# One decoder layer on one core: 192 transfers of the mixer issued from GpSimd's queue in place of the sync engine's

## The chip, the cores and the metric

The kernel runs on one core of one Trainium2 chip. Its time is the device time of one execution in microseconds (us). The engines are TensorE (PE, with its weight loads as PEld), VectorE (DVE), ScalarE (ACT), GpSimd (POOL) and the sync engine (SP). Each has a queue of its own, works through it in order, and waits at its head on semaphores. A DMA is issued by an instruction in one of these queues; its issue takes time on that engine, and the transfer then runs on the core's 16 DMA engines.

## The reference

One inference step of one layer, for 1024 prompt tokens and 8 sample tokens, all in float32: a half-step SwiGLU, a token mixer, cross-attention, a second half-step SwiGLU. The change lies in the mixer:

```python
proj = h @ P['w_in']                      # one projection, its columns split into the parts below
# RWKV-7 time mixing, 16 heads of 64: r, k, v, decay, a, g from token-shifted columns
S = S * w + sa * (kk * a) + v * k ;  y = S r            # per token, a scan over the prompt
rwkv_out = (groupnorm(y) + bonus) * g
# RG-LRU: conv of width 4, block-diagonal gates, linear scan
lru_out = hs * gelu(p_gelu)
gates = sigmoid(p_gate)
merged = gates[0] * rwkv_out + gates[1] * lru_out
out = merged @ P['w_mix_out']
h = layer_norm(alpha * h + out)
```

## The kernel before

Activations lie channels on partitions, 1032 columns wide (1024 prompt tokens and 8 samples). GEMMs take the columns in thirds of 344 (`CH3`). A float32 product is made of three matmuls on split operands (`mm3`, lines 122 to 127): a high part `HH` and a rest `HL` of the activations, `wh` and `wl` of the weights, which ACT and DVE split as the weights land in `raw` (lines 94, 99, 100).

The mixer's main loop runs over 16 units: 8 pairs of 128-channel tiles taken two at a time, each in 4 pieces of 256 or 264 tokens. For one unit there are small matmuls, ACT and DVE work and few POOL instructions: `stage` (token shift, norms, decays), `inverse` (a triangular solve), `chain` (the state carried from unit to unit, `ch`, `y`, `QZ`, `wsb`, lines 1105 to 1123) and `branch` (RG-LRU, lines 1005 to 1050, and the merge). POOL raises sums to the power -0.5 for the norms (`ivs`, `ivc`, line 798), copies `BN` (line 894), and does the same power in the samples (`v`, `w`, lines 1150 and 1220). A norm is a small matmul with ones (line 795), a DVE step, the power on POOL, ACT's scaling by the result, and a PE transposition of that (line 804).

Between these steps GEMMs are woven in as filler (`gemms`). `project` makes one 128-channel tile of the input projection: per third a GEMM into PSUM (`g`), an evacuation by ACT into `ev` (three buffers), and a store of it to DRAM `GD` (line 644), from where the units load it back later. The main loop makes 50 such tiles, 150 stores. The `lora` tiles, 18 stores ahead of the loop, go through the same line with `then` unset. Behind the last tile of the projection stands the output projection. `merged` loads the merged columns `MG` of a third, six 128-channel tiles, into `ev` (line 1241), and `direct` splits each into `HH` (ACT) and `HL` (DVE); `out_proj` multiplies them, eight output tiles by three thirds, 18 matmuls each, and stores the results to `FD` (line 1257). The buffers `ev` of project, merged and out_proj are the same three, used in turn.

What lies in each engine's queue, and in which order, is settled when the program is built: a scheduler takes the woven steps and puts each engine's instructions in order, also by which queue a transfer is issued from. Before the change SP issues all DMAs of the mixer: weights, the units' loads and stores (`T`, `D`, `GD`, `MG`), and the three named above.

Of the kernel before, what the change touches and what calls it, by code (L numbers as in the profile page):

```python
# [543 lines left out]
def mixer(octx, S, I, O, MG, HD, pre):  # L544
# [5 lines left out]
    nc, tc = S.nc, S.tc  # L550
# [7 lines left out]
    with ExitStack() as ctx:  # L558
# [66 lines left out]
        FD = S.dram.tile([8, 128, NT], F32, name="FD")  # L625
        GD = [S.dram.tile([128, 12, NT], F32, name="GD%d" % p) for p in range(8)]

        def cols(w, c0, n, q, kt=KT):
            yield from settled(S, c0, n)
            for k in range(kt):  # L630
                mm3(nc, q, wblock(w, k), S.HH[:, k, c0:c0 + n], S.HL[:, k, c0:c0 + n], k == 0, k == kt - 1)
                if k % 2:
                    yield

        def project(p, mt, gi, func, sc, w, cs, psg, pool, then=None):

            for c0, n in cs:
                q = psg(n)
                yield from cols(w, c0, n, q)
                if then:  # L640
                    then(c0, n)
                e = pool.tile([128, 344], F32, tag="ev", name="ev", bufs=3 if then else 2)[:, :n]
                ACT(e, q, func, scale=sc)
                nc.sync.dma_start(out=GD[p][:, gi, c0:c0 + n], in_=e)

        def tiles(p):

# [13 lines left out]
        def gemms():  # L661
# [18 lines left out]
            for j, (p, x, i) in enumerate(todo[:-1]):  # L680
                yield from project(p, *x, W[j], CH3, psg, t1, load)
                ready.add((p, x[1]))
                if i in (2, 5):
                    ends(p, i == 2)
# [4 lines left out]
            def then(c0, n):  # L689
                load(c0, n)  # L690
                merges.append(merged(c0, n))

            for _ in project(p, *x, W[len(todo) - 1], CH3, psg, t1, then):
                for m in merges:
                    next(m, 0)
                yield
            ready.update(((p, x[1]), "h"))
            yield from out_proj(W[len(todo):], load, merges)


        with ExitStack() as c2:
# [16 lines left out]
            def first():  # L718

                w = [S.ahead] + [load_split(S, I["w_in"][mt]) for mt in (25, *(x[0] for x in tiles(0)[:2]))]  # L720
                for cs in ([c] for c in CH3):
                    for i in range(2):
                        yield from low_in(i, w[i], cs)
                    for i in range(2):
                        yield from project(0, *tiles(0)[i], w[2 + i], cs, psl, lp)
# [62 lines left out]
        def tmp(tag, n=264, bufs=1, pool=None):  # L788
            return (pool or (t1 if tag in LATE else ta)).tile([128, n], F32, tag=tag, name=tag, bufs=bufs)
# [265 lines left out]
        def direct(k, c0, n, e):  # L1055

            ACT(S.HH[:, k, c0:c0 + n], e)
            TTo(S.HL[:, k, c0:c0 + n], e, S.HH[:, k, c0:c0 + n].bitcast(F32), ALU.subtract)
# [175 lines left out]
        def merged(c0, n):  # L1234

            for k in range(KT - 2):
                while not all(("mg", k, j) in ready for j in range(5) if c0 < (NT if j == 4 else 256 * j + 256) and
                              256 * j < c0 + n):
                    yield
                e = tmp("ev", 344, 3)[:, :n]  # L1240
                nc.sync.dma_start(out=e, in_=MG[k, :, c0:c0 + n])
                direct(k, c0, n, e)
                if k % 2:
                    yield

        def out_proj(W, load, merges):

            for m in range(KT):
                for j, (c0, n) in enumerate(CH3):
                    if m == 0:  # L1250
                        yield from merges[j]
                    q = psg(n)
                    yield from cols(W[m], c0, n, q, KT - 2)
                    load(c0, n)
                    e = tmp("ev", 344, 3)[:, :n]
                    ACT(e, q, scale=1.0 / ALPHA)
                    nc.sync.dma_start(out=FD[m, :, c0:c0 + n], in_=e)

        def out_last(n, w, st_, tags=(("g", 2),)):

# [63 lines left out]
        for t in range(nu):  # L1324
            g, n = divmod(t, 4)
# [417 lines left out]
```

## Time and profile before

| | us |
|---|---|
| median of three runs | 3201.08 (3195.89 to 3203.86) |
| profiled execution | 3202.45, its span 3200.7 |
| PE busy | 3015.8 (94%) |
| DVE busy | 2198.6 (69%) |
| ACT busy | 1434.0 (45%) |
| POOL busy | 558.1 (17%), 526 instructions |
| mixer's main loop with projection tiles as filler | about 850 to 1840 |
| first merged load to the last of them split | 1841 to 1917 |
| DMAs, all of one hardware kind of queue | 382.69 MB, 40.4% of 16 engines' span |

A busy time is the sum of an engine's instructions, register, branch and DMA-issuing instructions left out. An engine's busy share is a mean over stages, so the windows below are read stage by stage. The clock is the one granted to TensorE, as a share of 2.4 GHz. The profiled execution lies 1.4 us over the median.

### The profile page before, as it was taken

Reading aid. Unit: us, or ns where it says so; the run is one execution under the profiler, and the core shown is the slowest. Engines: PE = TensorE matmul, PEld = TensorE weight load, DVE = VectorE, ACT = ScalarE, POOL = GpSimd, SP = SyncE. Lnnn points to the kernel's source line nnn. Section 1 sums busy time; section 2 is a strip of 40 time slices with the busy share of each in tenths; the row PEclk is TensorE's granted clock in tenths of the full one; section 3 lists DMA queues with packets and bytes.
Section 4 is the critical chain, followed back from the end, with each engine's and each line's share of the span. In section 5 each row is a group of like instructions: output and inputs, shape, how many; then the busy total and the mean of one; then the engine's idle time right before and its main releaser. Section 6 shows DMA issues by size and latency. Waiting matters only on the chain. (4 is left out here: it accounts for less than half of the span.)

```text
span 3200.7 us, 63254 instructions
## 1 busy us (share of the span) xinstructions
PE 3015.8 (94%) x23324; PEld 2848.3 (89%) x23324; DVE 2198.6 (69%) x5903; ACT 1434.0 (45%) x3195; POOL 558.1 (17%) x526
## 2 busy tenths in 40 slices
PE   8999999999999999999999979889897999999997
PEld 8999999999888888888878858778887999999997
DVE  7666665574366887777777877776678666666556
ACT  5333352125465565556455655364235433334212
POOL 2222200132010011010001000260005322220111
PEclk9999999999999999999998969899999999999998
DMA  4222253314644554545554455554543222225321
GB/s 138 80 80 78 79 162 107 111 48 140 205 126 132 148 145 137 137 126 155 138 146 115 129 140 153 172 181 128 153 120 125 71 80 80 80 80 159 107 86 54
DMA packets 391301, 386.72 MB, mean 121 GB/s; under 512 B 153904, under 2 KB 292176, under 8 KB 390992
## 3 DMA queue, kind: packets, MB, share of 16 engines
q1 hardware_dynamic: 390992, 382.69, 40.4%
q8 instruction: 183, 3.00, 0.4%
q14 instruction: 126, 1.03, 0.1%
HBM read 277.54 MB, written 105.23 MB: 120 GB/s over the span
## 5 line engine op out<-in xcount | busy, mean ns | idle before, releaser
L125 PE MATMUL ps<-HH,wh 128*128 128x258 f32 (+1 forms) x2384 | 718.6, 302 | 18.7 <-ACT HH L510 7.8
L126 PE MATMUL ps<-HL,wh 128*128 128x258 f32 (+1 forms) x2384 | 716.7, 301 | 0.0
L127 PE MATMUL ps<-HH,wl 128*128 128x258 f32 (+1 forms) x2384 | 715.7, 300 | 0.0
L125 PE MATMUL g<-HH,wh 128*128 128x344 f32 (+2 forms) x1840 | 624.5, 340 | 15.9 <-DVE ql L1435 4.2
L127 PE MATMUL g<-HH,wl 128*128 128x344 f32 (+2 forms) x1840 | 596.8, 325 | 1.0 <-DVE wl L100 1.0
L126 PE MATMUL g<-HL,wh 128*128 128x344 f32 (+2 forms) x1840 | 594.3, 324 | 0.6 <-POOL HL L215 0.4
L125 PEld LDWEIGHTS ps<-HH,wh 128*128 128x128 f32 x2384 | 451.4, 189 | 21.0 <-ACT HH L510 7.8
L126 PEld LDWEIGHTS ps<-HL,wh 128*128 128x128 f32 x2384 | 451.2, 189 | 0.4 <-DVE HL L511 0.3
L127 PEld LDWEIGHTS ps<-HH,wl 128*128 128x128 f32 x2384 | 450.4, 189 | 0.0
L125 PEld LDWEIGHTS g<-HH,wh 128*128 128x128 f32 x1840 | 357.1, 194 | 35.3 <-DVE ql L1435 5.5
L126 PEld LDWEIGHTS g<-HL,wh 128*128 128x128 f32 x1840 | 357.7, 195 | 5.3 <-POOL HL L215 1.4
L127 PEld LDWEIGHTS g<-HH,wl 128*128 128x128 f32 x1840 | 356.1, 194 | 5.1 <-DVE wl L100 1.3
L228 ACT ACTIVATE wh<-raw 128x512 fp32r<-128x512 f32 x280 | 176.4, 631 | 322.2 <-PE ps L126 262.7
L334 POOL TENSOR_TENSOR raw<-raw 128x512 f32<-128x512 f32 x160 | 214.0, 1337 | 566.6 <-DVE wl L229 383.2
L229 DVE TENSOR_TENSOR wl<-raw,wh 128x512 fp32r<-128x512 f32 x280 | 206.7, 739 | 138.6 <-ACT wh L228 131.8
L100 DVE TENSOR_TENSOR wl<-raw,wh 128x512 fp32r<-128x512 f32 x302 | 218.6, 731 | 100.6 <-ACT wh L99 98.3
L99 ACT ACTIVATE wh<-raw 128x512 fp32r<-128x512 f32 x302 | 184.6, 625 | 222.5 <-PE ps L126 76.0
L442 DVE SCALAR_TENSOR_TENSOR acc<-ps,acc 128x344 f32<-128x344 f32 x336 | 168.4, 512 | 141.1 <-PE ps L127 140.4
L551 DVE TENSOR_TENSOR pr<-tq,iv 128x2 f32<-128x2 f32 (+30 forms) x496 | 160.8, 324 | 3.2
L556 ACT ACTIVATE ev<-g 128x344 f32<-128x344 f32 x192 | 86.9, 453 | 136.8 <-PE g L127 132.0
L949 DVE TENSOR_REDUCE tq<-pr 128x1 f32<-128x2 f32 (+30 forms) x496 | 121.8, 246 | 2.9
L556 ACT ACT_TABLE_LOAD x93 | 119.3, 1283 | 6.9 <-DVE cs L551 2.9
(404 smaller groups left out, 6302.8 us busy)
## 6 DMA issues: line engine op xcount, KB each, us to landing
raw<-in_wi_dram SPq DMA_DIRECT2D x176, 256.0 KB, 2.9
raw<-in_w_in_dram SPq DMA_DIRECT2D x116, 256.0 KB, 3.2
GD<-ev SPq DMA_DIRECT2D x168, 172.0 KB, 1.9
raw<-in_wo_dram SPq DMA_DIRECT2D x104, 256.0 KB, 2.8
raw<-HID SPq DMA_DIRECT2D x88, 258.0 KB, 3.6
HID<-g SPq DMA_DIRECT2D x80, 258.0 KB, 2.3
tg<-GD SPq DMA_DIRECT2D x32, 512.0 KB, 4.0
wt<-T SPq DMA_DIRECT2D x160, 64.0 KB, 2.9
```

What stands on the lines that cost most here:

```text
L99: nc.scalar.activation(out=hi, in_=raw, func=AF.Identity)
L100: S.low.tensor_tensor(out=lo, in0=raw, in1=hi.bitcast(F32), op=ALU.subtract)
L125: nc.tensor.matmul(ps, wh, xh, start=first, stop=False)
L126: nc.tensor.matmul(ps, wh, xl, start=False, stop=False)
L127: nc.tensor.matmul(ps, wl, xh, start=False, stop=last)
L228: nc.scalar.activation(out=hi, in_=x, func=AF.Identity)
L229: nc.vector.tensor_tensor(out=lo, in0=x, in1=hi.bitcast(F32), op=ALU.subtract)
L334: pool_tt = lambda o, a, b, op: nc.gpsimd.tensor_tensor(out=o, in0=a, in1=b, op=op)
L442: nc.vector.scalar_tensor_tensor(out=a, in0=q, scalar=0.5 / ALPHA, in1=a, op0=ALU.mult, op1=ALU.add)
L551: TTo = lambda o, a, b, op: nc.vector.tensor_tensor(out=o, in0=a, in1=b, op=op)
L556: ACT = lambda o, a, f=AF.Identity, **kw: nc.scalar.activation(out=o, in_=a, func=f, **kw)
L949: nc.vector.tensor_reduce(out=tq[:, 0:m, i], in_=pv, axis=mybir.AxisListType.X, op=ALU.add)
```

## The change

At three places of the mixer the DMA is issued from `nc.gpsimd` and no longer from `nc.sync`: the 150 stores of projection tiles in the main loop, the 18 loads of merged columns, and the 24 stores of the output projection, 172 KB each. The 18 stores of the lora tiles stay on SP. No instruction of another kind is added or taken away, but the scheduler gives every engine a new order.

```diff
@@ project
-                nc.sync.dma_start(out=GD[p][:, gi, c0:c0 + n], in_=e)
+                (nc.gpsimd if then else nc.sync).dma_start(out=GD[p][:, gi, c0:c0 + n], in_=e)
@@ merged
-                nc.sync.dma_start(out=e, in_=MG[k, :, c0:c0 + n])
+                nc.gpsimd.dma_start(out=e, in_=MG[k, :, c0:c0 + n])
@@ out_proj
-                    nc.sync.dma_start(out=FD[m, :, c0:c0 + n], in_=e)
+                    nc.gpsimd.dma_start(out=FD[m, :, c0:c0 + n], in_=e)
```

POOL's queue before, where the mixer turns from the input to the output projection:

```order
L798 TENSOR_TENSOR ivc<-ivc,mhalf 128x4
L798 TENSOR_TENSOR ivs<-ivs,mhalf 128x4
L894 COPY BN<-BN 64x4x64
L798 TENSOR_TENSOR ivc<-ivc,mhalf 128x4
L798 TENSOR_TENSOR ivs<-ivs,mhalf 128x4
L798 TENSOR_TENSOR ivc<-ivc,mhalf 128x4
L894 COPY BN<-BN 64x4x64
```

And after, at the same place (the first `ivc` and `ivs` here are the first two above):

```order
L798 TENSOR_TENSOR ivc<-ivc,mhalf 128x4
L1241 DMA ev<-MG 128x344 x2
L644 DMA GD_8811<-ev 128x344
L1241 DMA ev<-MG 128x344
L798 TENSOR_TENSOR ivs<-ivs,mhalf 128x4
L1241 DMA ev<-MG 128x344 x4
L644 DMA GD_8811<-ev 128x344
L1241 DMA ev<-MG 128x344 x4
L894 COPY BN<-BN 64x4x64
L1241 DMA ev<-MG 128x344
L644 DMA GD_8811<-ev 128x344
L1257 DMA FD<-ev 128x344
```

Loads four to seven of the merged columns now stand right behind the power `ivs`, and eight to eleven behind one store of the projection and ahead of the `BN` copy.

DVE's queue before, from the third merged column's split on: the three splits `HL<-ev` are followed by work of the units, and the fourth split stands 36 rows further down, as the second piece shows.

```order
L551 TENSOR_TENSOR HL<-ev,HH 128x344 x3
L552 SCALAR_TENSOR_TENSOR ysb<-ysb,tg 128x256
L1107 COPY wsb<-ch 128x128
L552 SCALAR_TENSOR_TENSOR ysb<-tg,ysb 128x256
L552 SCALAR_TENSOR_TENSOR s_23208<-x_23138,vec,x_23135 128x256
...
L551 TENSOR_TENSOR SC_23495<-sc,mask 128x512
L551 TENSOR_TENSOR wt<-wt,sv 128x256
L551 TENSOR_TENSOR SC_23500<-sc,mask 128x512
L551 TENSOR_TENSOR HL<-ev,HH 128x344
L551 TENSOR_TENSOR ws<-ws,wt 128x256
L551 TENSOR_TENSOR HL<-ev,HH 128x344 x2
```

And after, the same queue from the ninth row behind the three splits on:

```order
L551 TENSOR_TENSOR lm<-lm,gi 128x8
L551 TENSOR_TENSOR HL<-ev,HH 128x344
L551 TENSOR_TENSOR bv<-x_23204,m 128x256
L551 TENSOR_TENSOR HL<-ev,HH 128x344
L551 TENSOR_TENSOR cs<-cs,ref 128x256
L1040 COPY hl<-lm 128x9
L552 SCALAR_TENSOR_TENSOR xc<-cb,vec,xc 128x256
L875 COPY dend<-cs 128x4
L551 TENSOR_TENSOR lm<-lm,ge 128x264
L552 SCALAR_TENSOR_TENSOR xc<-cb,vec,xc 128x256
L551 TENSOR_TENSOR HL<-ev,HH 128x344
L552 SCALAR_TENSOR_TENSOR lm<-ge,lm 128x264
```

The fourth to sixth split, with which the first GEMM of the output projection can start, stand 10 to 19 rows behind the first three, where they stood 36 to 39 rows behind them.

## Rows read from the trace of the kernel before

**Rows 1.** Windows of the core: PE, PEld, DVE, ACT, POOL busy, clock, DMA.

```profile
850.00:1840.00 990.00, 934.04 (x7826) 832.01 (x7825) 743.17 (x2570) 572.82 (x1307) 99.07 (x96) 0.97 0.50 137
1840.00:1920.00 80.00, 60.30 (x441) 47.13 (x439) 59.91 (x192) 42.48 (x96) 6.15 (x6) 0.68 0.51 141
1920.00:2030.00 110.00, 96.59 (x736) 85.12 (x734) 80.65 (x256) 58.64 (x131) 8.07 (x7) 0.89 0.49 137
```

**Rows 2.** Waits of PE, 850 to 2030: total us, times, longest.

```profile
PE m L804 <- ACT s L556: 19.0, 13, 4.0
...
PE y L804 <- ACT gsq L556: 8.1, 8, 1.9
PE ch L1110 <- DVE wsb L1107: 6.7, 3, 5.8
```

**Rows 3.** Waits of SP's queue, 850 to 2030: total us, times, longest.

```profile
SPq L644 <- ACT ev L556: 130.7, 63, 5.2
SPq L1176 <- DVE pr L551: 31.0, 11, 12.9
...
SPq L655 <- DMA GD<-ev: 3.7, 5, 1.3
```

**Rows 4.** Waits of ACT, 880 to 2030, behind transfers: total us, times, longest.

```profile
ACT wh L99 <- DMA raw<-in_w_in_dram: 7.2, 6, 2.3
...
ACT xc L556 <- DMA cb<-GD: 5.9, 7, 2.8
```

**Rows 5.** Groups on POOL, 850 to 1840: busy us, mean ns, idle before.

```profile
L798 POOL TENSOR_TENSOR ivs<-ivs,mhalf 128x4 f32<-128x4 f32 x29 | 30.2, 1042 | 334.2 <-DVE ivs L554 119.2 <-DMA R<-GD 106.1 <-DVE tq L949 30.1
L798 POOL TENSOR_TENSOR ivc<-ivc,mhalf 128x4 f32<-128x4 f32 x24 | 24.6, 1023 | 308.1 <-DVE ivc L554 264.6 <-ACT QZ L556 30.2 <-DVE tq L949 8.6
L894 POOL COPY BN<-BN 64x256 f32<-64x256 f32 x29 | 19.6, 675 | 278.5 <-DVE BN L552 166.6 <-DVE tq L949 64.4 <-DVE pr L551 47.4
```

**Rows 6.** One copy on POOL in the timeline: start us, duration us.

```profile
1219.33 2.50 POOL L894 COPY BN<-BN 64x256 f32<-64x256 f32 x1 [10.60 <-DVE BN L552]
```

**Rows 7.** Line 644 on SP: issue min/median/max in ns.

```profile
L644 SPq DMA_DIRECT2D GD<-ev x168: 319/338/1736, 745.0 to 1882.8; - x168
```

**Rows 8.** Line 1241 on SP: issue min/median/max in ns.

```profile
L1241 SPq DMA_DIRECT2D ev<-MG x18: 319/378/597, 1841.4 to 1912.4; - x18
```

**Rows 9.** Timeline of SP's queue at the turn to the output projection.

```profile
1844.05 0.32 SPq L1241 DMA_DIRECT2D ev<-MG  x1
...
1850.49 2.54 SPq L954 DMA_DIRECT2D D<-tq  x4
...
1860.88 1.50 SPq L1241 DMA_DIRECT2D ev<-MG  x3
...
1892.62 0.94 SPq L1241 DMA_DIRECT2D ev<-MG  x2
1906.41 0.58 SPq L1176 DMA_DIRECT2D wt<-T  x1
1907.04 0.60 SPq L1241 DMA_DIRECT2D ev<-MG  x1
```

**Rows 10.** Timeline of DVE, three of the splits; idle before in brackets.

```profile
1852.63 1.36 DVE L551 TENSOR_TENSOR HL<-ev,HH 128x344 fp32r<-128x344 f32 x3
...
1870.85 0.52 DVE L551 TENSOR_TENSOR HL<-ev,HH 128x344 fp32r<-128x344 f32 x1 [0.33 <-ACT HH L556]
```

**Rows 11.** Timeline of PE at the turn to the output projection.

```profile
1836.13 0.32 PE L127 MATMUL g<-HH,wl 128*128 128x344 f32 x1
1836.29 0.32 PE L125 MATMUL g<-HH,wh 128*128 128x344 f32 x1
...
1854.58 0.69 PE L1110 MATMUL ch<-wsb,TT 64*64 64x64 f32 x8 [5.76 <-DVE wsb L1107]
...
1871.67 0.49 PE L126 MATMUL g<-HL,wh 128*128 128x344 f32 x1
1871.95 0.49 PE L127 MATMUL g<-HH,wl 128*128 128x344 f32 x1
```

## The prediction, made before the changed kernel ran

> **What bounds the kernel now.** I read the busy time in windows first, then the waits, then the timelines of one place. PE is busy for 94% of the span. In the mixer's main loop, 850 to 1840 us, it is busy for 934.04 of 990 us at a clock of 0.97 [rows 1]: 56 us idle in 16 units, so a transfer that comes earlier or later there has little to win. In the 80 us behind it, where the kernel turns to the output projection, PE is busy for 60.30 of 80 us, and the clock is 0.68; DVE has 59.91 us of work in them [rows 1]. That stretch is the one with slack.
>
> Next I ask what PE waits for. The largest waits are for normed tiles from ACT, `s` with 19.0 us in 13 waits and `gsq` with 8.1 us in 8 [rows 2]; both hang on the powers that POOL makes. SP waits for much longer at line 644, 130.7 us in 63 waits for ACT's evacuation [rows 3], and everything behind it in SP's queue waits along. But the consumers hardly feel it: the two largest waits of ACT for a transfer are 7.2 us for weights and 5.9 us for `cb` [rows 4], over more than 1100 us.
>
> **What an issue costs on POOL.** SP issues a store in 0.338 us and a load in 0.378 us (medians) [rows 7, 8]. No DMA is issued from POOL in this profile, so its price c per transfer is not seen. The lower bound is SP's 0.32 us. The upper one is the longest copy of POOL in a stretch of its timeline, 2.50 us [rows 6]. Between them I take 1.0 us, near to POOL's smallest operation, the power of four numbers a partition in 1.02 to 1.04 us [rows 5], whose length is nearly all fixed cost. The Trainium skill ("DMA: Bandwidth & Descriptors", specifications) gives about 1 us to the first byte for a DMA from GpSimd, against 0.6 us from the sync engine; by that c would be an estimated 1 us too. No run here shows it.
>
> **Part 1, 150 stores in the loop: a loss of 2.9 us.** POOL is busy for 99.07 of 990 us with 96 operations [rows 1], 53 of them powers [rows 5], so its queue has room: at c = 1.0 the stores fill 150/990, or 15%. What counts is that a power finds a store ahead of it. A store waits at POOL's head until ACT has evacuated the tile; the powers behind it wait too. That second kind of delay I put at nothing, as the tile is evacuated as soon as its GEMM ends and the GEMM stands ahead of the norm's matmul in PE's queue; if the scheduler's order breaks that, rival B grows. For the first kind an operation meets a store with a chance of 0.15 c and then loses c/2 on average: 96 x 0.15 c x c/2 = 7.3 c2 (c squared) of lateness. Of 53 powers 21 ended a wait of PE [rows 2, 5], so I let 0.4 of it through: 2.9 c2. That is 0.3 us at c = 0.32, 2.9 at 1.0 and 18 at 2.5.
>
> **Part 2, SP's queue freed in the loop: a gain of 1 us.** The 130.7 us of SP's waits go. The gain is at most what others wait for landings, 13 us in the two largest rows, and most of those transfers were late for other causes (a weight load is limited by its buffer, `cb` by its own producer). I take 1 us, between 0 and 4.
>
> **Part 3, the turn to the output projection: a gain of 12.3 us.** The first three merged columns are loaded by 1844.05 and split on DVE at 1852.63, in 1.36 us for all three [rows 9, 10], so their buffers are free at 1853.99. The next three loads are issued at 1860.88 only, 6.9 us later, behind the units' loads of line 954 and others that SP has to issue first [rows 9]. The sixth split runs at 1870.85, and the first GEMM of the output projection right behind it; two of its matmuls stand at 1871.67 and 1871.95 [rows 10, 11]. The last third meets the same thing again: SP issues two loads at 1892.62, then stands at line 1176 until 1906.41, 12.9 us behind DVE's `pr`, and issues the next load at 1907.04 [rows 3, 9]. Meanwhile PE has nothing but the chain's small matmuls, of which one waits for 5.76 us [rows 11].
>
> In the new order the loads are in a queue in which they pass SP's line 954 and 1176, and DVE's splits four to six stand 10 to 19 rows behind the first three instead of 36 to 39. So PE gets GEMM matmuls to put between the chain's waits. What can be won: 19.7 us of idle time in the 80 us [rows 1], and the slow clock. GEMM matmuls there start 0.28 us apart, against 0.16 at the full clock [rows 11]; 44 of them run so in the three thirds, 44 x 0.13 = 5.7 us. Together 25.4 us. DVE's 59.91 us of work set a floor, which leaves 20.1 us at most [rows 1]. The chain still passes between PE and DVE step by step, and no GEMM hides a wait when none is ready; I take 16 us of the 20.1, near the upper end as the GEMMs now are ready, with 0 as the lower end. From it goes POOL's slower issue: 18 loads at c - 0.38 each, a third of it on the path (one load of each three starts the split): 6 (c - 0.38), or 3.7 us at c = 1.0. Net 12.3 us. The 24 stores of the output projection I cost at nothing: their data is wanted only after 2030.
>
> **Sum.** 2.9 - 1 - 16 + 3.7 = -10.4 us. From the profiled execution's 3202.45 us that is 3192.05, and with 1.4 us for its distance to the median 3190.7, so **3191 us**. As a function of the price: 2.9 c2 - 17 + 6 (c - 0.38), which is -17 us at c = 0.32 (3184) and zero at c = 1.75. With the gain of part 3 between 12 and 20 instead of 16, and c between 0.5 and 1.3, the forecast's own range is 3182 to 3199.
>
> **Rival A, nothing to be measured, 3201 us.** Loads that come earlier only move the wait: the turn is a ping-pong of chain and DVE, and DVE with 59.91 us of work in 80 [rows 1] now does its splits ahead of the chain's copies, whose lateness was 5.76 us in one case already [rows 11]. What the output projection wins there the chain loses, and the last unit ends when it did. SP may also wait at its line 655, which loads back what line 644 stores (3.7 us in 5 waits [rows 3]), now until POOL has issued that store; the change would then only move the wait. For it speaks that most of a kernel's reordered work cancels out; against it, that PE is idle and slow for a reason that the loads can mend. Range 3194 to 3208. The Trainium skill speaks for it too ("DMA: Bandwidth & Descriptors", "Issuing engines are not separate DMA queues"): all issuers feed the same 16 engines, and a second one saves only the issue time, which is usually small. SP's rows agree on the size (0.338 us), but the waits ahead of an issue that they show are another thing.
>
> **Rival B, slower, 3220 us.** POOL becomes the gate of the norms. If c is near 2.5 us, 38% of POOL's time in the loop is issue: 18 us of lateness reach PE. At the turn, powers, projection stores and 18 loads share one queue, and the loads cost 6 x 2.12 = 12.7 us; only half of part 3's gain stays, 8 us. The sum is 18.1 - 1 - 8 + 12.7 = +21.8 us, 3223; between that and the break-even at 1.75 I put 3220. It decides the sign from c = 1.75 on. For it: PE's largest waits already hang on POOL's powers [rows 2], and its copies vary up to 2.50 us [rows 6]. Against it: the powers and most copies end in about 1 us or less [rows 5]. The Trainium skill has a mechanism for a high price ("SBUF — State Buffer", "SBUF: two separate sides"): a DMA from GpSimd needs its cores to write descriptors, and some VectorE operations lock them out of a port they share. DVE is busy for three quarters of the loop [rows 1]; the copy's 2.50 us against a mean of 0.675 fits such a lock, but no row here shows it on a DMA.
>
> **Rival C, a larger gain, 3177 us.** c is as small as on SP, part 3 gives all 20.1 us, and SP's freed queue gives 4 us in the loop: 3201.05 - 24.1 = 3177.
>
> **How the numbers follow.** I give the forecast 0.44, A 0.26, B 0.20 and C 0.10. A change within 0.3% (9.6 us, 3191.5 to 3210.7) can't be told from none here. The forecast lies at that edge: of its 0.44 I count 0.25 as faster, 0.18 as the same, 0.01 slower. A gives 0.05, 0.18 and 0.03; B 0.01 the same and 0.19 slower; C 0.10 faster. Together 0.40, 0.37 and 0.23. The range of 3174 to 3219 leaves out the better half of C and the worse part of B.
>
> **What would show it.** The price c: the durations of lines 644, 1241 and 1257 on POOL. Part 1: waits of PE at line 804 above 27 us in all mean that stores delay the powers. Part 2: SP's waits at line 644 are gone, and ACT's waits for landings fall. Part 3: loads four to six are issued within 2 us of 1853.99's counterpart, the first GEMM of the output projection starts some 8 us earlier against the unit's chain, and the stretch from the first merged load to the last split takes some 12 us less with a higher clock. The prediction is wrong if c is above 1.75 us, if PE's idle time in the loop grows by more than a few us, or if that stretch stays 80 us long although its loads are early.

## The result and the profile after

The changed kernel takes 3175.95 us (median of 4 runs, 3173.59 to 3177.37) where the kernel before takes 3201.75 in the runs made beside it: a ratio of 0.9921, with a 95% interval from 0.9908 to 0.9935, or about 25 us. The forecast was 3191, with a range of its own from 3182 to 3199; the time lies within the outer range only, beside the figure of rival C (3177), whose parts were other ones.

First the windows of the changed kernel, as [rows 1] has them for the one before. The columns are PE, PEld, DVE, ACT and POOL busy, the granted clock, and the DMA engines' share and GB/s. POOL's column now counts its DMA issues too (255 entries where there were 96).

```profile
850.00:1840.00 990.00, 928.50 (x7911) 829.00 (x7910) 763.48 (x2633) 586.03 (x1332) 192.30 (x255) 0.97 0.51 142
1840.00:1920.00 80.00, 73.31 (x532) 60.48 (x532) 64.53 (x208) 50.20 (x114) 18.13 (x28) 0.86 0.57 163
1920.00:2030.00 110.00, 96.26 (x841) 82.47 (x840) 72.55 (x228) 46.71 (x110) 23.15 (x29) 0.83 0.48 142
```

By these one would say that the turn to the output projection has become dense, as the prediction wanted. But the same clock time is no longer the same work: the turn begins 32 us earlier (the first merged load at 1809.21 instead of 1841.4). So I cut both traces at points of the program: the first `TN` transposition of the first unit on DVE (line 970), that of the thirteenth unit, and the last copy to `wsb` (line 1107). First the kernel before, then the changed one; each in one window of twelve units, and one from there to the end of the chain.

```profile
952.90:1795.61 842.71, 796.47 (x6858) 707.23 (x6859) 645.69 (x2230) 485.83 (x1120) 84.95 (x82) 0.96 0.50 137
...
1795.61:2052.87 257.26, 220.17 (x1728) 185.25 (x1727) 187.66 (x609) 132.11 (x298) 25.81 (x26) 0.83 0.51 142
```

```profile
955.86:1771.46 815.60, 774.13 (x6841) 690.73 (x6840) 643.29 (x2223) 484.56 (x1113) 158.39 (x206) 0.98 0.51 141
...
1771.46:2024.02 252.56, 219.05 (x1742) 183.87 (x1742) 186.04 (x610) 131.69 (x303) 53.65 (x76) 0.85 0.50 144
```

Twelve units of the loop take 27.1 us less, and all the rest of the mixer 4.7 us less. Of the 27.1 us, 4.8 are PE's idle time (842.71 - 796.47 = 46.2 against 41.5) and 22.3 are PE's busy time, for as good as the same number of matmuls (6858 and 6841): they run at a higher clock, 0.98 in place of 0.96. Cut into stretches of 4 us, the loop before has 11 places where the clock is below full, which together lose 30.7 us (one minus the clock, times the length), the loop after has 5, which lose 13.6. So the clock accounts for 17 of the 22.3 us; what makes up the rest was not looked into. What such a place looks like is seen in the kernel before, on PE, at 1677; two windows and then the timeline with its idle times in brackets:

```profile
1658.00:1674.00 16.00, 15.98 (x153) 14.41 (x153) 5.93 (x20) 4.53 (x12) 1.01 (x1) 1.00 0.82 218
1674.00:1690.00 16.00, 12.13 (x67) 9.89 (x67) 12.68 (x62) 8.39 (x22) 2.79 (x3) 0.68 0.31 90
```

```profile
1677.22 0.61 PE L795 MATMUL m<-ones,s 128*128 128x2 f32 x4 [1.46 <-ACT s L556]
...
1679.71 0.69 PE L804 MATMUL m<-ident,s 128*128 128x128 f32 x2 [1.03 <-ACT s L556]
...
1684.34 0.49 PE L125 MATMUL g<-HH,wh 128*128 128x344 f32 x1
1684.63 0.49 PE L126 MATMUL g<-HL,wh 128*128 128x344 f32 x1
```

Up to 1674 PE is busy for 15.98 of 16 us at a clock of 1.00. It then waits for 1.46 us, the clock falls, and around further waits (1.03 us is the longest) it runs its GEMM at 0.29 us a matmul, the lower of the clock's two levels (1.2 GHz; at 2.4 GHz a matmul took 0.16 [rows 11]), until the clock is back. In these 16 us the waits are 3.9 us and the clock loses 5.1 (0.32 x 16): the matmuls behind a few short waits cost more than the waits themselves.

The price of an issue on POOL and the transfers' way, by the sources of the two lines (min/median/max in ns) and the page's part on queues:

```profile
L644 POOL DMA_DIRECT2D GD<-ev x150: 539/542/731, 865.3 to 1846.3; - x150
```

```profile
L1241 POOL DMA_DIRECT2D ev<-MG x18: 536/536/614, 1809.2 to 1869.5; - x18
...
DMA to landing us min/median/max: 2.5/3.4/6.2
```

```profile
q1 hardware_dynamic: 363344, 348.86, 37.3%
q0 software_dynamic: 12288, 33.83, 3.0%
```

Against SP's 0.338 and 0.378 us [rows 7, 8] a transfer costs 0.54 us on POOL, by the duration that the profile gives. They go through a queue of their own kind.

SP's waits for ACT's `ev` at line 644 and 1257, 130.7 us before [rows 3] for the first, are gone. In their place SP waits elsewhere. Three rows of the changed kernel, 850 to 2000, the first two in front of the weights' loads (line 94), the third for stores that POOL issued:

```profile
SPq L94 <- DVE tq L949: 46.6, 23, 5.6
SPq L94 <- DVE wl L100: 35.1, 20, 8.2
...
SPq L655 <- DMA GD<-ev: 20.0, 8, 5.7
```

SP does not stand for less time by this. Over the twelve units the sum of all its waits is 414.7 us before and 448.8 in the changed kernel; what differs is where it stands. Before, 114.9 us of it are for `ev` at line 644, with whatever comes next in the queue behind them; now 90.7 us are at line 94, where they were 27.0.

The turn itself, on DVE, POOL and PE, answering to [rows 9 to 11]:

```profile
1829.28 1.36 DVE L551 TENSOR_TENSOR HL<-ev,HH 128x344 fp32r<-128x344 f32 x3
...
1837.05 0.52 DVE L551 TENSOR_TENSOR HL<-ev,HH 128x344 fp32r<-128x344 f32 x1 [0.60 <-ACT HH L556]
```

```profile
1830.32 1.74 POOL L1241 DMA_DIRECT2D ev<-MG  x3 [7.07 <-DVE HL L551]
...
1863.72 1.12 POOL L798 TENSOR_TENSOR ivs<-ivs,mhalf 128x4 f32<-128x4 f32 x1 [0.78 <-DVE ivs L554]
1864.80 0.61 POOL L1241 DMA_DIRECT2D ev<-MG  x1
```

```profile
1831.23 0.70 PE L1110 MATMUL ch<-wsb,TT 64*64 64x64 f32 x8 [6.86 <-DVE wsb L1107]
...
1835.94 0.65 PE L125 MATMUL g<-HH,wh 128*128 128x344 f32 x1 [2.04 <-ACT ev L556]
1836.39 0.49 PE L126 MATMUL g<-HL,wh 128*128 128x344 f32 x1
1836.68 0.49 PE L127 MATMUL g<-HH,wl 128*128 128x344 f32 x1
```

The kernel before began the same GEMM here:

```profile
1871.21 0.66 PE L125 MATMUL g<-HH,wh 128*128 128x344 f32 x1 [0.26 <-ACT ev L556]
```

Loads four to six are issued while the first splits end, where SP was 6.9 us late, and the output projection's first GEMM begins 35.3 us earlier. Of these, 23.4 are the whole chain's being earlier (its matmul behind the longest wait, line 1110, starts at 1831.23 instead of 1854.58), and 11.9 are won against the chain. The chain's own wait in front of that matmul has not shrunk: 6.86 us where it was 5.76 [rows 11]. And the GEMM still begins at the lower clock (0.29 us a matmul), as before.

### The profile page after: what moved, and what is told of

Its sections match the earlier page's. It is cut to its first block, busy times and chain, and to the rows that moved or that the text cites. A ratio compares the mean times of both kernels' runs of the same rounds, so it can differ in the third digit from the quotient of the medians.

```text
span 3171.8 us, 63384 instructions
## 1 busy us (share of the span) xinstructions
PE 2997.5 (95%) x23324; PEld 2835.5 (89%) x23324; DVE 2196.4 (69%) x5903; ACT 1433.0 (45%) x3193; POOL 669.7 (21%) x718
## 3 DMA queue, kind: packets, MB, share of 16 engines
q0 software_dynamic: 12288, 33.83, 3.0%
## 5 line engine op out<-in xcount | busy, mean ns | idle before, releaser
L644 POOL DMA_DIRECT2D GD<-ev x150 | 84.4, 563 | 632.5 <-ACT ev L556 411.8
L464 POOL TENSOR_TENSOR acc<-acc,raw 128x516 f32<-128x516 f32 x32 | 42.7, 1340 | 420.0 <-DVE acc L442 322.4
```

What stands on the lines that cost most here:

```text
L644: (nc.gpsimd if then else nc.sync).dma_start(out=GD[p][:, gi, c0:c0 + n], in_=e)
```

## The experiments

Each was timed in five rounds beside the kernel before. The table has the ratio with its interval, and from the profiled execution the twelve units (before 842.7, changed 815.6) and the rest to the last `wsb` copy (257.3 and 252.6).

| | what | median us | ratio (95%) | twelve units | rest |
|---|---|---|---|---|---|
| changed | all three on POOL | 3175.95 | 0.9921 (0.9908 to 0.9935) | 815.6 | 252.6 |
| e1 | only the 150 stores on POOL | 3179.3 | 0.9937 (0.9922 to 0.9951) | 817.0 | 247.3 |
| e2 | only merged loads and output stores on POOL | 3188.03 | 0.9964 (0.9952 to 0.9976) | 839.0 | 249.3 |
| e3 | only the 150 stores, on ACT | 3177.82 | 0.9933 (0.9917 to 0.995) | 812.4 | 264.7 |
| e4 | changed, SP made to wait at each store | 3200.67 | 1.0004 (0.9985 to 1.0022) | 843.9 | 255.2 |
| e5 | changed, each store in two halves | 3173.37 | 0.9913 (0.9892 to 0.9933) | 820.4 | 251.9 |
| e6 | before, stores recorded later | 3217.68 | 1.0052 (1.0036 to 1.0069) | 847.7 | 265.8 |
| e7 | before, 18 lora stores on POOL | 3204.2 | 1.0008 (0.9997 to 1.002) | 844.0 | 256.1 |
| e8 | changed, SP issues 150 more without that wait | 3177.2 | 0.9927 (0.9911 to 0.9944) | 825.2 | 254.2 |
| e9 | changed in its exact order, SP waits | 3186.0 | 0.9955 (0.9942 to 0.9968) | 824.0 | 248.9 |
| e10 | changed, 88 more stores on POOL | 3177.56 | 0.993 (0.9916 to 0.9944) | 830.6 | 238.2 |
| e11 | the 150 stores on ACT, the rest on POOL | 3171.19 | 0.9902 (0.9888 to 0.9916) | 806.5 | 248.4 |

A single profiled execution lies up to 9 us off its kernel's median (e5 and e11), so smaller differences between rows of the last two columns say little.

**e1, the stores alone.** The first line of the diff was kept, the other two undone.

```diff
-                nc.gpsimd.dma_start(out=e, in_=MG[k, :, c0:c0 + n])
+                nc.sync.dma_start(out=e, in_=MG[k, :, c0:c0 + n])
```

> Only the 150 stores of the projection are issued from GpSimd; merged loads and output-projection stores stay on SP. After the change the loop's twelve first units (first to thirteenth TN transposition on DVE) took 815.6 us where they took 842.7, and the rest to the last wsb copy 252.5 where it took 257.3. Theory Q (SP's queue no longer stands behind its wait at line 644, so the units' transfers come earlier): the loop keeps its gain, twelve units in 813 to 820 us, total 3176 to 3184. Theory O (the new order of PE, DVE and ACT is what helps, by fewer gaps behind which the clock falls; its size is chance): the loop's order is nearly that of the changed kernel, so the same, and this run does not tell Q from O. The prediction as written (turn 12 us, loop -2): total about 3203.

The loop keeps its gain, and the total most of it. What the prediction had put at a loss of 1.9 us (its parts 1 and 2) is a gain of about 20.

**e2, the loads and output stores alone.** The reverse.

```diff
-                (nc.gpsimd if then else nc.sync).dma_start(out=GD[p][:, gi, c0:c0 + n], in_=e)
+                nc.sync.dma_start(out=GD[p][:, gi, c0:c0 + n], in_=e)
```

> Only the 18 merged loads and 24 output-projection stores are issued from GpSimd; the 150 stores stay on SP. The prediction as written: the turn gains some 12 us, total about 3189. Q and O: the first twelve units stay at 842 us within 2, and the total falls by 3 to 6 us, to 3195 to 3199.

A gain of 0.36%, or 11.5 us by the ratio: part 3's 12.3 us were right for this edit alone. The two gains do not add: 20 and 11.5 against 25 together. In e1 the rest already takes 10 us less with all loads still on SP; why, was not followed up. Theories Q and O had 3195 to 3199 for e2 and were wrong in that.

**e3, ACT in place of POOL.**

```diff
-                nc.sync.dma_start(out=GD[p][:, gi, c0:c0 + n], in_=e)
+                (nc.scalar if then else nc.sync).dma_start(out=GD[p][:, gi, c0:c0 + n], in_=e)
```

> The 150 stores are issued from ScalarE's queue, right behind the evacuation, everything else as before the change. SP is freed of the same waits, POOL has nothing new, ACT pays about 0.34 us each, some 50 us. Q: the twelve units gain 15 to 27 us as in the changed kernel (less what ACT's issue costs), total 3178 to 3192. O: the order is a third one, differing from both by about as much; the total may lie anywhere from 3180 to 3215.

The loop gains as much, though POOL has nothing new. So the gain hangs on SP being rid of the stores, not on POOL's having them.

**e4, SP made to wait again.** The stores stay on POOL; SP stores one partition of the same buffer to a place that nobody reads.

```diff
+        GX = S.dram.tile([168, 344], F32, name="GX"); gx = itertools.count()
...
+                then and nc.sync.dma_start(out=GX[(x_ := next(gx)):x_ + 1, :n], in_=e[0:1, :])
```

> The changed kernel, and SP issues beside each of the 150 stores a small one of one partition from the same buffer to an unused place, so that SP stands behind ACT's evacuation as before. Q: SP's waits of over 100 us at line 644 are back and the loop's gain goes, twelve units in 835 to 845 us, total 3195 to 3205. O: SP's waits are back but the time is not tied to them; total anywhere from 3170 to 3205, twelve units likely below 835.

The gain is gone: 1.0004. That is more than the loop's 20 us: e4 keeps the edits at the turn, which gave 11.5 us by themselves in e2. Some of its loss is therefore something other than what SP stands behind in the loop, and what it is no run separates. SP's largest wait, by its row:

```profile
SPq L644 <- ACT ev L556: 144.1, 70, 5.6
```

**e5, the price on POOL doubled.** Each store goes in two halves of 172 columns; PE's order hardly differs from the changed kernel's.

```diff
+                [(nc.gpsimd if then else nc.sync).dma_start(out=GD[p][:, gi, c0 + o:c0 + o + h], in_=e[:, o:o + h])
+                 for o, h in (((0, 172), (172, 172)) if then else ((0, n),))]
```

> The changed kernel with each of the 150 stores issued as two halves, so that POOL pays about 1.08 us a third where it pays 0.54; the order of the other engines stays close to the changed kernel's. By the prediction's term 2.9 c squared the loss goes from 0.8 us to 3.4 us: 3177 to 3181. If POOL's queue is the gate of the norms (rival B) the loss is 8 us or more and the waits of PE at line 804 grow by as much. If POOL has room, within 2 us of the changed kernel.

```profile
L644 POOL DMA_DIRECT2D GD<-ev x300: 539/539/731, 865.7 to 1854.7; - x150
```

Another 0.54 us for every third, 81 us more of POOL, cannot be measured. The 2.6 us that the formula gives would be lost in the noise; the 8 us or more of rival B would hardly be. POOL has room.

**e6, stores recorded later, on SP.**

```diff
+                hold.append((c0, n, e))     # store all but the newest; at a tile's last third, all
+                [nc.sync.dma_start(out=GD[p][:, gi, c_:c_ + n_], in_=e_) for c_, n_, e_ in ...]
```

> The kernel before, its 150 stores still on SP, but a third's store is recorded behind the next third's evacuation (the last two of a tile together), so that for two of three the data is ready long before SP comes to it. Theory Q (SP's standing behind the evacuation is what costs): SP's waits at line 644 fall to below half of 115 us in the loop, and the twelve units take 820 to 832 us, total 3180 to 3192. Theory P (what costs is the number of transfers that SP has to issue, 0.34 us each, in the order as planned): no gain, 3197 to 3205.

This missed its aim, and it is slower by 0.5%, outside what either theory had. SP's waits for `ev` at line 644 fell, from 114.9 us to 84.5, and yet the time rose by some 16 us. A shorter wait alone did not help here, and a new order can cost that much; whether it is the order or the buffer, which is held longer, was not followed up.

**e7, a new order by itself.**

```diff
+                (nc.sync if then else nc.gpsimd).dma_start(out=GD[p][:, gi, c0:c0 + n], in_=e)
```

> The kernel before, with only the 18 lora stores ahead of the loop on GpSimd; the 150 stores stay on SP. The order of the engines changes in 547 places of PE (654 where only the 150 stores move), so it shows what a new order alone does. Theory O (any new order moves the time by tens of us): the twelve units differ from 842.7 us by 8 or more in either direction. Q and P: 838 to 847 us, total 3197 to 3205.

No change: an order shuffled in a like number of places, with SP standing at line 644 as before, is worth nothing. One such sample does not exclude a lucky order, and e6 shows that a new order can move the time. What speaks more clearly against luck is the table as a whole. In the five kernels in which SP waits for `ev` at line 644 (before, e2, e4, e6, e7), the twelve units take 839.0 to 847.7 us; in the seven in which the order was made without that wait (changed, e1, e3, e5, e8, e10, e11), 806.5 to 830.6.

**e8, as many issues, other wait.** As e4, but the small store reads the tile's weights, which are split long before.

```diff
+                then and nc.sync.dma_start(out=GX[(x_ := next(gx)):x_ + 1, :n], in_=w[0][0].bitcast(F32)[0:1, :n])
```

> The changed kernel, and SP issues beside each of the 150 stores a small one of one partition, from the tile's weights, which are split long before; so SP has as many transfers to issue as with the waits kept, but does not stand behind ACT's evacuation. Q: the gain stays, twelve units 813 to 822 us, total 3174 to 3183. P: the gain goes as it did with the waits kept, 835 to 850 us, total 3195 to 3203.

The total keeps the gain, though the units take 825.2 us, 3 us over what Q had allowed; SP now stands 29.7 us behind ACT's `wh`. Against e4 what SP's small store reads and waits for differs (and the order, settled anew for each), and 23 us lie between them. So it is this wait for `ev`, not the number of transfers. That e4's small store reads `ev`, too, before it can be used again is not excluded as a part of its loss, but ACT has no wait for that store.

**e9, the wait without a new order.** How does this wait reach PE? In the loop the waits of ACT for landing transfers are 15.7 us before and 14.4 after, those of DVE 2.3 and 5.8: transfers are hardly late for anyone in either. So I left every engine's instructions in the changed kernel's order, and gave SP only the wait, after the order had been settled: the transfer next behind a store's place waits for ACT's count as the store does.

```diff
+    for i in ins:                      # all instructions, in the order settled
...
+        if ...Pool and "GD" in str(i.outs[0]) and "ev" in str(i.ins[0]):
+            todo = ...                 # the store's wait on ACT
+        elif ...SP and todo is not None:
+                _BI(i).wait_op(_bass.SemaphoreHandle(todo.ant_name, todo.id), todo.wait_value, "sem-ge", False)
```

> The changed kernel, every engine's instructions in exactly its order, the stores on GpSimd; only that the transfer which SP issues next behind a store's place in the program waits for the same evacuation too, at about 145 places. So SP stands again, but nothing was ordered anew for it. If the standing costs at run time (theory QR), SP's waits of over 80 us for ACT's ev in the loop are back, and 15 us or more of the gain go: 3190 to 3203, waits for landing transfers on ACT and DVE grow by 8 us or more. If the standing costs through the order that is planned around it (theory QP), the time stays within 6 us of the changed kernel's: 3172 to 3182.

It lies between the theories: 3186.0, so by the medians 10 us of the 26 go and 16 stay (by the ratios 11 and 14). The waits are back, the largest ones now in front of other lines:

```profile
SPq L940 <- ACT ev L556: 39.5, 11, 5.6
SPq L94 <- ACT ev L556: 32.0, 16, 5.5
```

In all SP waits for `ev` for 206.3 us from 950 to 1800, where it was 114.9 before the change. ACT's waits for landings rise from 14.4 to 34.7 us, above all for weights:

```profile
ACT wh L99 <- DMA raw<-in_w_in_dram: 16.7, 16, 2.6
```

And the twelve units:

```profile
959.10:1783.10 824.00, 777.91 (x6841) 693.97 (x6841) 643.83 (x2224) 486.63 (x1113) 157.49 (x206) 0.98 0.50 140
```

PE's idle time is back at 46.1 us, as before the change, but its busy time is 777.91 us and not 796.47, at a clock of 0.98 and not 0.96. In 4 us stretches the clock loses 17.1 us, near the 13.6 of the changed kernel and far from the 30.7 before: as much idle time, but in this order the clock falls less. Of the 27.1 us that the units had gained, 18.7 stay.

**e10 and e11, further versions.** e10 moves the stores of lines 863, 1050 and 1084 to POOL as well; e11 joins e3's stores on ACT with the loads and output stores on POOL.

```diff
-            nc.sync.dma_start(out=GD[p][:, GB, c0:c0 + 256], in_=bv)
+            nc.gpsimd.dma_start(out=GD[p][:, GB, c0:c0 + 256], in_=bv)
```

> The changed kernel, and 88 more stores of the mixer (lines 863, 1050 and 1084) moved from SP to GpSimd. They wait for DVE and ACT as the moved ones do. If any standing of SP costs, some 5 to 10 us more are gained: 3166 to 3172. If GpSimd's powers now meet stores that wait for DVE, a loss of 3 to 15 us: 3179 to 3190.

> The 150 stores on ScalarE's queue, merged loads and output stores on GpSimd. The loop as with the stores on ScalarE alone (812 us for twelve units), the turn as with the merged loads moved: 3168 to 3176, if the two gains add as the loop and the turn are apart; 3176 to 3184 if the turn gives nothing.

e10 gains nothing: the loop takes 830.6 us, ACT waits longer for the powers on POOL (for `ivc` 48.3 us, in the changed kernel 39.9), and 18.8 us for the stores of line 1084 to have read their buffer:

```profile
ACT gsq L556 <- POOL ivc L798: 48.3, 19, 4.3
...
ACT ysb L556 <- DMA MG<-ysb: 18.8, 9, 3.0
```

e11 has the lowest median of all, 3171.19 us. Its interval overlaps that of the changed kernel, so that it beats the kernel before is shown, and that it beats the changed one is not.

## Why the prediction was right in its outer range and wrong in its sum

**Direction and outer range** (3174 to 3219) held; the forecast's own range (3182 to 3199) did not. The sum of -10.4 us stands against -25.8; it is part 2 that failed. As most of the gain came from a part that the sum had at 1 us, that the time lies within the outer range, 2 us from its lower end, is luck more than insight.

**Part 1** (the stores on POOL cost 2.9 us at c = 1.0): the price is 0.54 us, near the lower bound of 0.32, and by its own formula the loss is 0.8 us. e5 shows that even twice the price cannot be seen in the time. The choice of c = 1.0 misread its rows: POOL's copy of `BN` at 0.675 us is shorter than the power [rows 5], and the power's length is not nearly all fixed, as that of eight numbers takes 1.74 us (line 1150). The 0.4 rests on unlike windows, 21 waits of PE up to 2030 (for ACT, which waits for the powers) against 53 powers up to 1840. PE's waits at line 804 did rise, from 27.1 us to 32.9:

```profile
PE m L804 <- ACT s L556: 25.1, 13, 3.6
...
PE y L804 <- ACT gsq L556: 7.8, 9, 1.9
```

The prediction wanted to read this as delay by stores. But with the stores doubled (e5) they are 32.7 (22.0 + 10.7), no more. The stores do seem to hold the powers up: over the twelve units ACT's waits for POOL are 45.5 us before, 73.9 in the changed kernel and 82.5 in e5, against 58.9 in e3, where POOL has no stores. But this is spent ahead of PE, all of whose waits together are 45.9, 41.3, 39.5 and 36.1 us. How much of it is the second kind of delay, which the prediction put at nothing, was not separated. Rival B needed c = 1.75. The mechanism that I cited for it from the Trainium skill ("SBUF — State Buffer", "SBUF: two separate sides") did not show: with DVE busy for 763.48 of the 990 us the slowest of 150 issues took 0.731 us. The figure of about 1 us to the first byte ("DMA: Bandwidth & Descriptors", specifications) was no price for the issue: an issue took 0.54 us on POOL.

**Part 2** (SP's freed queue gives 1 us, at most 4): it gives about 20 (e1, e3), and with SP put back behind the evacuation the whole gain is gone (e4). This was the mis-sized term. The step that failed is "the gain is at most what others wait for landings". It reads the wait where it is booked, and ACT's waits for landings hardly moved (15.7 to 14.4 us). The transfers did come earlier: from the issue of a weight load (line 94) to its split on ACT (line 99), both taken in their order, the median of 81 in the units is 6.6 us before, 7.7 in the changed kernel, 6.6 in e4 and 5.5 in e9. Presumably a transfer that is late in a plan made around it makes nobody wait. By e9 some 10 us come back when SP stands behind the evacuations without a new order, as idle time of PE and later weights, and that with more of this wait than there was. Some 16 us stay, which include what the turn gives; in the loop they go with the order that the scheduler makes when SP does not have the stores, and mostly with PE's clock. That the plan counts SP's wait, by which of its choices it packs PE better, and what the order before would gain from a freed SP, no run shows; that stays open.

**Part 3** (the turn gives 12.3 us): right for its edit alone, 11.5 us by e2; in the changed kernel, behind part 2, about 5 are left of it. Why the two overlap is not shown; at the turn itself, from 1835 to 1900, SP stood at line 644 for 6.6 us. Loads four to six and the splits came as said, the first GEMM 11.9 us earlier against the chain where some 8 were said. The price of the slow clock was slightly off (0.28 - 0.16 is 0.12, so 5.3 us and not 5.7, and its 44 matmuls stand in no row), which the floor of 20.1 us hides. The stretch from the first merged load to the last split fell from 75.5 us to 67.0, so by 8.5 us in place of some 12, first before, then changed:

```profile
1841.38:1916.87 75.49, 55.78 (x412) 43.70 (x410) 56.60 (x182) 40.21 (x91) 6.15 (x6) 0.66 0.50 140
...
1809.20:1876.17 66.97, 52.58 (x358) 42.02 (x359) 49.76 (x151) 38.23 (x90) 16.48 (x28) 0.72 0.60 165
```

The clock rose from 0.66 to 0.72 only: the low clock at the turn was not mended.

**Rival A** drew on the rule of the Trainium skill ("DMA: Bandwidth & Descriptors", "Issuing engines are not separate DMA queues") that a second issuer saves only the issue time. Here it takes a wait ahead of the issue out of SP's queue, and e8 shows that the issue time itself (150 more transfers on SP) is worth next to nothing in the total. Two of rival A's own mechanisms did show, without costing the gain: SP's wait at line 655 rose from 3.7 to 20.0 us, and the chain's wait of 5.76 us became 6.86. **Rival C** had the total by luck, with 20 us at the turn and 4 in the loop; it was the other way round.

## What to carry to other kernels

A store that waits for its producer at the head of a queue which also carries loads can cost what no consumer's wait shows. The sum of that queue's waits does not show it either, as it rose here while the time fell. Look for what stands in front of the loads, and try the store on an engine with room before weighing the price of an issue. Where a scheduler orders all engines, a change of queue is a change of every order: undo the queue and the order apart, as e9 does, before telling a story of one wait. And on PE count busy time at equal work beside idle time, as most of a gain may be clock (here 17 of 27.1 us in the loop).

## What the runs showed of the hardware that was not expected

By the profile an issue of a 172 KB transfer takes 0.54 us on POOL (median 0.542, longest 0.731 of 150), against 0.326 us on ACT (e3) and 0.338 on SP; halves of it cost the same 0.539 each (e5), so here the price is per transfer and not per byte. The 192 moved transfers appear as 12288 packets of the software queue, 64 for each, where the hardware queue has 27648 packets less than before, 144 for each.
